# A decoder step on one core: a modulation unit multiplied in three visits instead of two, fewer constant products, and a later broadcast

## The chip, the cores and the metric

The kernel runs on one core of a Trainium2 chip. The metric is the device time in microseconds (us); of three runs of the kernel before, the median is 1660.69 us (1659.94 to 1660.98). TensorE (PE) multiplies, VectorE (DVE), ScalarE (ACT) and GpSimd (POOL) work elementwise, and SyncE (SP) issues nearly all DMA transfers, in its program order.

## What is computed

One inference step of a one-layer decoder for 288 tokens (256 of a prompt, 8 requests of 4 tokens), 2048 features. Only its beginning matters here: a conditioning vector per request is turned into shifts and scales by `w_ada`, the tokens are normalised and modulated, and the result is multiplied by `w_in`.

```python
mod = (jax.nn.silu(c) @ w_ada + b_ada).reshape(n, N_MOD, 1, D_MODEL)
sh_m, sc_m, gt_m, sh_f, sc_f, gt_f = [mod[:, i] for i in range(N_MOD)]
h = _rms(x, g_mix) * (1 + sc_m) + sh_m        # _rms: x * rsqrt(mean(x*x) + EPS) * gain
proj = h @ w_in
...                                           # convolution mixer and gating mixer, merged
x = x + gt_m * (merged @ w_out)
h2 = _rms(x, g_ffn) * (1 + sc_f) + sh_f
gate, up = jnp.split(h2 @ w_ffn_in, 2, axis=-1)
x = x + gt_f * ((jax.nn.silu(gate) * up) @ w_ffn_out)
```

## The kernel before

Tokens lie along the free dimension (288 columns); features lie in 16 tiles of 128 partitions. All weights, some 350 MB in float32, are read once, so a long stream of weight blocks is loaded while PE multiplies. Each float32 weight is split into a rounded part `hi` (a cast on ACT) and the rest `lo` (a subtraction on DVE), and a product is three matmuls: hi by hi, hi by lo, lo by hi.

The list `steps` is the order of the program. Its members are the following.

- **Units of modulation** (`Ada`, matmuls on L344): `aA` (4 loads of 512 KB) gives scale and shift of feature tile 0, `aB` (8 loads of 768 KB) those of tiles 1 to 3, `aC` those of tiles 4 to 7 (8 loads of 1 MB). A *visit* is a run of a unit's loads that PE multiplies one after another. All loads of a unit accumulate in one PSUM bank, and `tail` turns it into rows of `mod`. PE reads the raw data, so its buffer is free once PE has read it.
- **Blocks of `wA`** (matmuls on L448 for block 0, the class `FirstBlk`, and on L430 to L432 for blocks 1 to 8): feature tile 0 times eight output tiles each, 512 KB each. Blocks 0 to 5 use the raw x of tile 0 times its scale and are multiplied by the row factor later, on POOL (`rescale`); blocks 6 to 8 use the normalised tile 0, `h1[0]`. The raw buffer of a block is free once ACT and DVE have split it.
- **Blocks of `wB`, `wC`, `wE`, `wD`** and the rest of the layer follow.
- **The row factor**: `squares` (on ACT or POOL) of the 16 tiles of x, `sums1` (L504), which adds them up on PE, `sums1_out` and `rstd1` (L525, L528), and `norm1`, which broadcasts the row factor on PE (L202) and copies it to the tile `rb` (ACT).
- **`warm(n)`** (L234): n products of a constant tile of ones with itself, whose result nobody reads.

Five raw buffers (`RAW = 5`) serve the whole stream. At each step the load of the stream's member five places ahead is issued on SP; it waits until a buffer is free. Everything behind it on SP waits too.

Results of PE go to four PSUM accumulators `pm`. Each output tile of a block is copied out, odd ones by ACT and even ones by DVE (`sinkA`). Work that is to lie between the output tiles is hung on them by `at(block, j3=[...])`: it is issued behind the copy of tile 3. In this way each block also carries the splitting of the next one, `high` behind tiles 1 and 5, `low` behind tiles 2 and 6. `V` and `A` are pinned: DVE and ACT keep the written order here, so a copy can stand behind a cast that waits for a load.

Of the kernel before, what the change touches and what calls it, by code (L numbers as in the profile page):

```python
# [23 lines left out]
SEG = 4  # L24
# [52 lines left out]


def _body(tc, nc, d, pc, pw, pslot, ptmp, pps):
    ids = [0]  # L80

    def nm(s):
        ids[0] += 1
        return f"{s}_{ids[0]}"
# [4 lines left out]
    def slot(dt=F32, shape=(P, T)):  # L89
        return pslot.tile(list(shape), dt, tag="s", name=nm("s"), padded_shape=[P, TU])  # L90
# [29 lines left out]
    V, A, G, PE, SY = Pinned(nc.vector), Pinned(nc.scalar), nc.gpsimd, nc.tensor, nc.sync  # L120
# [18 lines left out]
    def load_x(a, b):  # L139
        SY.dma_start(x[:, a:b, :], d["x"][:, a:b, :])  # L140

    def load_consts():
        SY.dma_start(cp, d["cpack2"])
        SY.dma_start(masks[96:], d["cpack2"][:32, C_MASKS : C_MASKS + 32])
# [80 lines left out]
    def in_order(i):  # L225
        if S["strict"]:
            S["pe"] = i
        return i

    def warm(n, after=None):  # L230
        ps = psmisc()
        with behind(after):
            for _ in range(n):
                PE.matmul(ps[:, :P], ones, ones, start=True, stop=True)  # L234
# [82 lines left out]
    class Ada(Step):  # L317
# [15 lines left out]
        def run(self):  # L333
            w, ks = self.nq * 128, self.ks
            if self.blk == 0:
                Ada.cur[self.name] = pps.tile([P, 512], F32, tag="ada", name=nm("ada"), bufs=1)
            acc = Ada.cur[self.name]
            for k in range(self.nk // ks):
                for j in range(4):
                    kt = self.blk * self.nk + k * ks + j % ks  # L340
                    o = (k * 4 + j) * w
                    with behind(S.get("pe")):
                        self.last = in_order(
                            PE.matmul(  # L344
                                acc[32 * j : 32 * j + 32, :w],
                                cs[:, kt, :],
                                self.raw[:, o : o + w],
                                start=(kt < ks),
                                stop=(kt >= 16 - ks),
                                tile_position=(0, 32 * j),  # L350
                                skip_group_check=True,
                            )
                        )
            if (self.blk + 1) * self.nk == 16 and not self.defer:
                self.tail()
# [80 lines left out]
    class FirstBlk(Blk):  # L436
        def run(self):
            ah, al = self.rhs(0)
            g = SEG
            for m0 in range(0, self.nm, g):  # L440
                pss = [psmain() for _ in range(g)]
                for n in range(3):
                    for i, ps in enumerate(pss):
                        wh, wl = self.parts[m0 + i]
                        w, a = ((wh, ah), (wl, ah), (wh, al))[n]
                        with behind(S.get("pe")):
                            self.last = in_order(
                                PE.matmul(ps[:, : self.n], w, a, start=n == 0, stop=n == 2)  # L448
                            )
                for i, ps in enumerate(pss):  # L450
                    self.sinks(m0 + i, ps)

    class KBlk(Blk):
        def run(self):
# [30 lines left out]
    def ada(name):  # L485
        u = units[name]
        return [Ada(u, b) for b in range(16 // u[3])]
# [4 lines left out]
    def square(k, eng):  # L492
        q = sq[k] = slot()
        if eng is A:
            A.activation(q, x[:, k, :], AF.Square)
        else:
            G.tensor_tensor(q, x[:, k, :], x[:, k, :], ALU.mult)
# [72 lines left out]
    def gain1(k0, k1):  # L570
        V.scalar_tensor_tensor(
            gm1[:, k0:k1, :],
            mod[:, 16 + k0 : 16 + k1, :],
            1.0,
            gmix[:, k0:k1].unsqueeze(2).to_broadcast([P, k1 - k0, NC]),
            ALU.add,
            ALU.mult,
        )
# [246 lines left out]
    aA, aB, aC, aE = (ada(n) for n in ("aA", "aB", "aC", "aE"))  # L825
    wA = [FirstBlk("wA", 0, xe.__getitem__, sinkA, TU)]
# [3 lines left out]
    wC = [Blk("wC", i, rh1, sinkC) for i in range(RAWX // 2)]  # L830
    wE = [Blk("wE", i, rh1, sinkC) for i in range(RAWX // 4, 18)]
    mo = [Modulate(k, gm1, 0, "rb1", h1) for k in range(16)]

    def at(blk, **acts):
        for j, f in acts.items():
            blk.then.setdefault(int(j[1:]), []).extend(f)
# [6 lines left out]
    wA[0].defer = wB[0].defer = True  # L843

    def squares(*ks):
        return [lambda k=k, e=(G if k in (3, 5, 7, 9, 10, 12, 14, 15) else A): square(k, e) for k in ks]

    at(wA[0], j3=squares(0, 3, 5), j7=squares(1))
    at(wA[1], j3=squares(2), j7=squares(4))
    at(wA[2], j3=squares(6, 7, 9, 10), j7=squares(8))  # L850
    at(wA[3], j3=squares(11, 12, 14, 15), j7=squares(13))
    at(wA[4], j0=[sums1_out], j2=[rstd1])
    at(wA[6], j0=[aB[-1].tail], j3=[lambda: gain1(1, 4)], j5=[mo[1].affine], j7=[mo[1].high])
    at(wA[7], j0=[mo[1].low], j3=[mo[2].affine], j6=[mo[2].high])
    at(wA[8], j0=[mo[2].low], j2=[mo[3].affine], j5=[mo[3].high], j6=[mo[3].low])
# [5 lines left out]
    def free():  # L861
        V.on = A.on = False

    def h1_0():
        mo[0].norm()
        mo[0].affine()
        mo[0].high()
        mo[0].low()

    def norms():  # L870
        for k in range(1, 4):
            mo[k].norm()

    steps = [Do(silu), Do(lambda: warm(17)), *aA[:2], Do(lambda: warm(3, aA[1].last)), aA[2]]
    steps += [Do(lambda: warm(2, aA[2].last)), aA[3], Do(lambda: warm(1, aA[3].last)), Do(aA[3].tail), Do(early0)]
    steps += [Do(lambda: warm(4, aA[3].last))] + wA[:4] + [Do(sums1), wA[4], Do(norm1)] + aB[:4] + [Do(h1_0), wA[5]]
    steps += aB[4:] + [Do(norms)] + wA[6:] + [Do(free), wB[0]] + aC[:4] + wB[1:3] + aC[4:]
    steps += [wB[3], gain(4, 8), mk_h1(4, 5), mk_h1(5, 6), wB[4], mk_h1(6, 7), mk_h1(7, 8), rescale(0, 8), wB[5]]
    steps += [rescale(8, RAWX)] + weave(wC, visits(aE, 4, gain(8, 16)), 1, 13)[:-6]
# [39 lines left out]
    n = len(steps)  # L919
# [14 lines left out]
    for s in steps:  # L934
        if isinstance(s, Do):
            s.run()
            continue
        i = pos[id(s)]
        if i + AHEAD < len(stream):
            nx = stream[i + AHEAD]  # L940
            nx.load()
            if nx in pieces:
                load_x(*pieces[nx])
            if nx is wA[3]:
                SY.dma_start(ident, d["cpack2"][:, C_ID : C_ID + P])
            if nx is wA[8]:
                load_consts()
        while (
            nxt < len(blks)
            and blks[nxt].raw is not None  # L950
            and nxt <= cur + 1
            and not (blks[nxt].defer and blks[nxt] is not s)
        ):
            blks[nxt].split()
            nxt += 1
        s.run()
        if isinstance(s, Blk):
            cur += 1
# [112 lines left out]
```

## Time and profile before

| | before |
|---|---|
| median of the runs | 1660.69 us |
| the profiled execution, time | 1661.07 us |
| the profiled execution, span | 1659.2 us |
| HBM read | 352.56 MB |

The span runs from the first to the last instruction; some 1.9 us lie around it. In the slices of the page (one digit is a tenth of busy time in a fortieth of the span, 41.5 us) PE shows 8 in the second slice, 7 in the last and 9 in all others:

```profile
PE   9899999999999999999999999999999999999997
PEclk9999999999999999999999999999999999999998
```

The second slice, from 41 to 83 us, holds idle time. The costliest groups are the three matmuls of a product, 3704 of each:

```profile
L430 PE MATMUL pm<-s,hi 128*128 128x288 f32 (+1 forms) x3704 | 1097.5, 296 | 8.6 <-ACT s L113 8.0
L431 PE MATMUL pm<-s,hi 128*128 128x288 f32 (+1 forms) x3704 | 1094.2, 295 | 0.3 <-DVE s L113 0.3
```

Behind the count stand busy time, mean ns of one, and the time for which the engine was idle just before them, with what ended it. Matmuls overlap, so 296 ns is the length of one and not the distance between two, which is 133 to 140 ns here.

### The profile page before, as it was taken

How to read it: one execution, taken by the hardware profiler on the slowest of the kernel's cores; microseconds unless marked ns; L12 is line 12 of the kernel's file. 1: busy time of each engine (PE TensorE's matmuls, PEld its weight loads, DVE VectorE, ACT ScalarE, POOL GpSimd, SP SyncE). 2: the span in 40 equal slices, each digit the busy share in tenths (PEclk: the TensorE clock that was granted, in tenths of full speed). 3: DMA queues.
4: the chain of work that ended last, by engine and by line, in shares of the span. 5: the costliest groups of instructions: out<-in, count | busy, mean ns of one | idle time of the engine just before them, and what ended most of it. 6: DMA issues, size and time to landing. Idle time of an engine off the chain costs nothing.

```text
span 1659.2 us, 31266 instructions
## 1 busy us (share of the span) xinstructions
PE 1634.1 (98%) x12472; PEld 1562.1 (94%) x12472; DVE 986.8 (59%) x1993; ACT 734.7 (44%) x1370; POOL 120.7 (7%) x251
## 2 busy tenths in 40 slices
PE   9899999999999999999999999999999999999997
PEld 7688899989898999999999899999999999999997
DVE  4575567877765557557844455555555555555565
ACT  4343344643344434446733344444444444444453
POOL 2059000010100000002300000000000000000000
PEclk9999999999999999999999999999999999999998
DMA  7877864566777776674466755444454444544352
GB/s 289 308 286 286 338 213 175 177 250 249 278 307 278 281 285 246 255 267 156 153 254 254 301 170 195 173 158 141 157 205 161 170 138 155 201 166 168 126 172 76
DMA packets 57473, 357.66 MB, mean 216 GB/s; under 512 B 6528, under 2 KB 8992, under 8 KB 25328
## 3 DMA queue, kind: packets, MB, share of 16 engines
q1 hardware_dynamic: 56976, 354.95, 58.5%
q8 instruction: 97, 1.59, 0.4%
q0 software_dynamic: 352, 0.73, 0.1%
q14 instruction: 48, 0.39, 0.1%
HBM read 352.56 MB, written 3.09 MB: 214 GB/s over the span
## 4 chain that ended last, share of the span: by engine, by line
issue 50%; DVE 0%; ACT 0%; PE 0%; POOL 0%; POOLq 0%; DVEq 0%
DVE x L113 0%; PE px L202 0%; ACT t L113 0%; POOLq L1057 0%; POOL t L275 0%; ACT hi L113 0%; ACT s L113 0%; DVEq L1057 0%; POOL t L276 0%
## 5 line engine op out<-in xcount | busy, mean ns | idle before, releaser
L430 PE MATMUL pm<-s,hi 128*128 128x288 f32 (+1 forms) x3704 | 1097.5, 296 | 8.6 <-ACT s L113 8.0
L431 PE MATMUL pm<-s,hi 128*128 128x288 f32 (+1 forms) x3704 | 1094.2, 295 | 0.3 <-DVE s L113 0.3
L432 PE MATMUL pm<-s,lo 128*128 128x288 f32 (+1 forms) x3704 | 1094.1, 295 | 0.3 <-DVE lo L113 0.2
L113 DVE TENSOR_TENSOR lo<-raw,hi 128x512 fp32r<-128x512 f32 (+1 forms) x972 | 659.8, 686 | 481.3 <-ACT hi L113 467.6
L113 ACT CAST hi<-raw 128x512 fp32r<-128x512 f32 (+1 forms) x972 | 583.7, 607 | 797.3 <-PE pm L431 653.4
L430 PEld LDWEIGHTS pm<-s,hi 128*128 128x128 f32 x3704 | 697.6, 188 | 28.1 <-issue 12.0
L432 PEld LDWEIGHTS pm<-s,lo 128*128 128x128 f32 x3704 | 697.0, 188 | 1.1 <-DVE lo L113 1.1
L431 PEld LDWEIGHTS pm<-s,hi 128*128 128x128 f32 x3704 | 697.2, 188 | 0.6 <-DVE s L113 0.6
L344 PE MATMUL ada<-raw,cs 128*32 128x512 f32 (+3 forms) x896 | 90.5, 540 | 1.1 <-DMA raw<-in_aC 1.1
L113 DVE TENSOR_TENSOR s<-pm,s 128x288 f32<-128x288 f32 x120 | 54.5, 456 | 39.0 <-PE pm L432 38.7
L344 PEld LDWEIGHTS ada<-raw,cs 128*32 128x32 f32 x896 | 26.3, 111 | 47.5 <-issue 42.5
L196 POOL TENSOR_TENSOR r<-r,mhalf 128x3 f32<-128x3 f32 x3 | 2.8, 923 | 865.7 <-DVE r L113 865.7
L113 DVE TENSOR_TENSOR s<-t,s 128x288 fp32r<-128x288 f32 (+1 forms) x109 | 51.2, 471 | 12.0 <-ACT s L113 11.9
L113 ACT CAST s<-t 128x288 fp32r<-128x288 f32 (+1 forms) x109 | 47.1, 433 | 20.8 <-DVE t L113 16.4
L113 DVE SCALAR_TENSOR_TENSOR t<-t,pm 128x288 f32<-128x288 f32 x84 | 37.9, 451 | 25.2 <-PE pm L432 25.2
L562 POOL TENSOR_TENSOR s<-s,rb 128x288 f32<-128x288 f32 x48 | 43.0, 896 | 0.0
L113 DVE SCALAR_TENSOR_TENSOR x<-pm,mod,x 128x256 f32<-128x256 f32 x80 | 38.0, 476 | 0.0
L113 DVE SCALAR_TENSOR_TENSOR s<-pm,s 128x288 f32<-128x288 f32 x48 | 24.6, 512 | 15.2 <-PE pm L432 15.0
L113 DVE TENSOR_TENSOR t<-pm,mod 128x32 f32<-128x32 f32 x80 | 15.4, 192 | 29.5 <-PE pm L432 29.4
L239 POOL TENSOR_TENSOR t<-x,gm 128x32 f32<-128x32 f32 x16 | 7.4, 462 | 323.7 <-DVE gm L113 278.5
L275 POOL TENSOR_TENSOR t<-s,gm 128x32 f32<-128x32 f32 x28 | 12.0, 427 | 173.9 <-DVE s L113 103.4
L113 DVE SCALAR_TENSOR_TENSOR s<-s,pm 128x288 f32<-128x288 f32 x32 | 14.5, 454 | 15.2 <-PE pm L432 15.2
(122 smaller groups left out, 519.9 us busy)
## 6 DMA issues: line engine op xcount, KB each, us to landing
raw<-in_fi SPq DMA_DIRECT2D x84, 1024.0 KB, 4.8
raw<-in_a SPq DMA_DIRECT2D x64, 1024.0 KB, 6.3
raw<-in_f SPq DMA_DIRECT2D x64, 704.0 KB, 4.1
raw<-in_wD SPq DMA_DIRECT2D x36, 1024.0 KB, 5.2
raw<-in_wC SPq DMA_DIRECT2D x24, 896.0 KB, 6.0
raw<-in_aE SPq DMA_DIRECT2D x16, 1024.0 KB, 8.7
raw<-in_wo SPq DMA_DIRECT2D x16, 1024.0 KB, 7.3
raw<-in_aC SPq DMA_DIRECT2D x8, 1024.0 KB, 7.9
```

The lines of the kernel that those rows point to most:

```text
L113: i = f(*args, **kw)
L196: G.tensor_tensor(r, r, mhalf, ALU.pow)
L239: G.tensor_tensor(sam(a[:, TP:T]), sam(x[:, k, TP:]), bc4(gm[:, k, 1:]), ALU.mult)
L275: G.tensor_tensor(sam(h[:, TP:]), sam(t[:, TP:]), bc4(gm[:, k, 1:]), ALU.mult)
L344: PE.matmul(acc[32 * j : 32 * j + 32, :w], cs[:, kt, :], self.raw[:, o : o + w], start=(kt < ks), stop=(kt >= 16 - ks), tile_position=(0, ...
L430: PE.matmul(ps[:, : self.n], wh, ah, start=first, stop=False)
L431: PE.matmul(ps[:, : self.n], wh, al, start=False, stop=False)
L432: self.last = in_order(PE.matmul(ps[:, : self.n], wl, ah, start=False, stop=last))
L562: G.tensor_tensor(a[:, :T], a[:, :T], S["rb1"], ALU.mult)
```

## The change

It has six parts, all in the first hundred microseconds. The unit `aB` is multiplied in visits of two, two and four loads (before block 4's sum of squares, behind block 4, behind block 5) instead of four and four (behind block 4, behind block 5). The sum of squares stands behind the first visit, the broadcast `norm1` behind the second. The normalisation of tile 0 for blocks 6 to 8 (`mo[0]`) is hung on the output tiles of block 5 instead of standing ahead of it. Block 0 takes its output tiles two together and then one by one, instead of four and four. The constant products are 10, 1, 2, 1, 5 instead of 17, 3, 2, 1, 4. The squares are dealt out anew, eight on POOL as before, and the constants' load (`cp`, 236 KB) is asked for at a later step.

```diff
     class FirstBlk(Blk):
         def run(self):
             ah, al = self.rhs(0)
-            g = SEG
-            for m0 in range(0, self.nm, g):
-                pss = [psmain() for _ in range(g)]
+            cuts = [0] + list(range(2, self.nm + 1))
+            for a, b in zip(cuts, cuts[1:]):
+                pss = [psmain() for _ in range(a, b)]
...
     def squares(*ks):
-        return [lambda k=k, e=(G if k in (3, 5, 7, 9, 10, 12, 14, 15) else A): square(k, e) for k in ks]
-
-    at(wA[0], j3=squares(0, 3, 5), j7=squares(1))
+        return [lambda k=k, e=(G if k in (6, 7, 8, 9, 10, 12, 14, 15) else A): square(k, e) for k in ks]
+
+    at(wA[0], j3=squares(0), j7=squares(1))
     at(wA[1], j3=squares(2), j7=squares(4))
-    at(wA[2], j3=squares(6, 7, 9, 10), j7=squares(8))
+    at(wA[2], j3=squares(3, 6, 7, 8), j7=squares(5, 9, 10))
     at(wA[3], j3=squares(11, 12, 14, 15), j7=squares(13))
     at(wA[4], j0=[sums1_out], j2=[rstd1])
+    at(wA[5], j0=[mo[0].norm], j2=[mo[0].affine], j4=[mo[0].high], j6=[mo[0].low])
...
-    def h1_0():
-        mo[0].norm()
-        mo[0].affine()
-        mo[0].high()
-        mo[0].low()
-
...
-    steps = [Do(silu), Do(lambda: warm(17)), *aA[:2], Do(lambda: warm(3, aA[1].last)), aA[2]]
+    steps = [Do(silu), Do(lambda: warm(10)), *aA[:2], Do(lambda: warm(1, aA[1].last)), aA[2]]
     steps += [Do(lambda: warm(2, aA[2].last)), aA[3], Do(lambda: warm(1, aA[3].last)), Do(aA[3].tail), Do(early0)]
-    steps += [Do(lambda: warm(4, aA[3].last))] + wA[:4] + [Do(sums1), wA[4], Do(norm1)] + aB[:4] + [Do(h1_0), wA[5]]
+    steps += [Do(lambda: warm(5, aA[3].last))] + wA[:4] + aB[:2] + [Do(sums1), wA[4]] + aB[2:4] + [Do(norm1), wA[5]]
     steps += aB[4:] + [Do(norms)] + wA[6:] + [Do(free), wB[0]] + aC[:4] + wB[1:3] + aC[4:]
...
-            if nx is wA[8]:
+            if nx is wC[1]:
                 load_consts()
```

SP, from the identity to block 7 of wA. First before: `raw_170` is block 4, `raw_493` block 5, `raw_601` block 6.

```order
L945 DMA ident<-in_cpack 128x128
L394 DMA raw_170<-in_wA 128x1024
L328 DMA raw_212<-in_aB 128x1536
L328 DMA raw_278<-in_aB 128x1536
L143 DMA cp<-in_cpack 128x472
L328 DMA raw_340<-in_aB 128x1536
L144 DMA masks<-in_cpack 32x32
L328 DMA raw_408<-in_aB 128x1536
L394 DMA raw_493<-in_wA 128x1024
L328 DMA raw_566<-in_aB 128x1536
```

The same place in the changed kernel, where `raw_266` is block 4 and `raw_468` block 5; `raw_161`, `raw_204`, `raw_328` and `raw_400` are the first four loads of aB.

```order
L940 DMA ident<-in_cpack 128x128
L328 DMA raw_161<-in_aB 128x1536
L328 DMA raw_204<-in_aB 128x1536
L394 DMA raw_266<-in_wA 128x1024
L328 DMA raw_328<-in_aB 128x1536
L328 DMA raw_400<-in_aB 128x1536
L143 DMA cp<-in_cpack 128x472
L394 DMA raw_468<-in_wA 128x1024
L328 DMA raw_475<-in_aB 128x1536
L328 DMA raw_498<-in_aB 128x1536
```

Two loads of aB have moved ahead of block 4, and `cp` from between aB's second and third load to behind the fourth.

PE, from block 4's last tile to block 5's first. Before, `pm_554` is block 4's tile 7 and `pm_603` block 5's tile 0:

```order
L432 MATMUL pm_554<-s_197,lo_466 128x298
L202 MATMUL px_560<-ident,r_519 128x128 x3
L344 MATMUL ada_568<-raw_212,cs 32x384 x4
L344 MATMUL ada_568<-raw_278,cs 32x384 x4
L344 MATMUL ada_568<-raw_340,cs 32x384 x4
L344 MATMUL ada_568<-raw_408,cs 32x384 x4
L430 MATMUL pm_603<-s_197,hi_509 128x298
```

In the changed kernel, where `pm_559` is block 4's tile 7 and `pm_585` block 5's tile 0:

```order
L432 MATMUL pm_559<-s_188,lo_458 128x298
L344 MATMUL ada_470<-raw_328,cs 32x384 x4
L344 MATMUL ada_470<-raw_400,cs 32x384 x4
L202 MATMUL px_577<-ident,r_524 128x128 x3
L430 MATMUL pm_585<-s_188,hi_514 128x298
```

Two of the four loads are left here, and the broadcast has gone behind them; the other two (`raw_161`, `raw_204`) now stand between block 3 and the sum of squares.

ACT, from the copy of the broadcast into block 5. Before, `hi_615` is the first half of block 6 and `s_629` the copy of block 5's tile 3:

```order
L113 COPY rb_564<-px_560 128x288
L113 ACTIVATE t_593<-s_591,mod,gm_90 128x256
L113 CAST s_597<-t_593 128x288
L113 COPY s_613<-pm_609 128x298
L113 CAST hi_615<-raw_601 128x512
L113 COPY s_629<-pm_625 128x298
```

In the changed kernel `hi_599` is the first half of block 6 and `s_617` the copy of tile 3:

```order
L113 COPY rb_581<-px_577 128x288
L113 COPY s_597<-pm_593 128x298
L113 CAST hi_599<-raw_583 128x512
L113 ACTIVATE t_609<-s_591,mod,gm_90 128x256
L113 COPY s_617<-pm_613 128x298
L113 CAST s_625<-t_609 128x288
```

The modulation of tile 0 (`ACTIVATE`, then the cast) has moved from ahead of block 5's copies to behind the cast of block 6.

More of the change, by code (lines that the diff above doesn't have):

```diff
@@ L438, in run @@
             ah, al = self.rhs(0)
-            g = SEG
-            for m0 in range(0, self.nm, g):
-                pss = [psmain() for _ in range(g)]
+            cuts = [0] + list(range(2, self.nm + 1))
+            for a, b in zip(cuts, cuts[1:]):
+                pss = [psmain() for _ in range(a, b)]
                 for n in range(3):
                     for i, ps in enumerate(pss):
-                        wh, wl = self.parts[m0 + i]
-                        w, a = ((wh, ah), (wl, ah), (wh, al))[n]
+                        wh, wl = self.parts[a + i]
+                        w, r = ((wh, ah), (wl, ah), (wh, al))[n]
                         with behind(S.get("pe")):
                             self.last = in_order(
-                                PE.matmul(ps[:, : self.n], w, a, start=n == 0, stop=n == 2)
+                                PE.matmul(ps[:, : self.n], w, r, start=n == 0, stop=n == 2)
                             )
                 for i, ps in enumerate(pss):
-                    self.sinks(m0 + i, ps)
+                    self.sinks(a + i, ps)
     class KBlk(Blk):
```

## The prediction

> **What bounds the kernel now.** I read the page first, then the windows, then the timeline of the one stretch in which TensorE stands still.
>
> ```profile
> span 1659.2 us, 31266 instructions
> PE 1634.1 (98%) x12472; PEld 1562.1 (94%) x12472; DVE 986.8 (59%) x1993; ACT 734.7 (44%) x1370; POOL 120.7 (7%) x251
> 200.00:1640.00 1440.00, 1439.82 (x10920) 1392.36 (x10913) 864.71 (x1755) 655.61 (x1206) 43.34 (x117) 1.00 0.57 205
> ```
>
> From 200 to 1640 us TensorE (PE) is busy for 1439.82 of 1440 us at full clock. No DMA, VectorE (DVE) or ScalarE (ACT) wait shows there, and the diff adds no product. So whatever start of that stretch moves, the end moves by the same amount. The change can act only in the first hundred microseconds.
>
> ```profile
> 34.00:36.00 2.00, 1.49 (x11) 1.25 (x9) 0.18 (x1) 0.83 (x3) 0.00 (x0) 1.00 0.02 8
> 36.00:38.00 2.00, 1.11 (x6) 0.87 (x7) 1.94 (x5) 1.28 (x4) 0.86 (x1) 1.00 0.00 0
> 38.00:40.00 2.00, 2.00 (x25) 0.99 (x27) 0.46 (x1) 0.93 (x2) 0.41 (x2) 1.00 0.48 89
> 44.00:46.00 2.00, 0.23 (x2) 0.00 (x0) 0.00 (x0) 0.00 (x0) 0.00 (x0) 1.00 0.98 399
> ...
> 43.94 0.29 PE L432 MATMUL pm<-s,lo 128*128 128x298 f32 x1
> 51.53 0.62 PE L430 MATMUL pm<-s,hi 128*128 128x298 f32 x1 [7.30 <-ACT s L113]
> 52.58 3.97 PE L344 MATMUL ada<-raw,cs 128*32 128x384 f32 x32
> 56.48 0.40 PE L430 MATMUL pm<-s,hi 128*128 128x288 f32 x1
> ...
> 50.55 0.62 ACT L113 CAST hi<-raw 128x512 fp32r<-128x512 f32 x1 [7.88 <-DMA raw<-in_wA]
> 51.08 0.71 ACT L113 COPY s<-pm 128x298 f32<-128x298 f32 x2
> ```
>
> In a window row the columns are length, busy time of PE, PE weight load, DVE, ACT and POOL, then granted clock, DMA share and GB/s. PE stops at 43.94 and resumes at 51.53: 7.3 us. It waits for ACT to empty an accumulator, and ACT, in program order, waits for the raw data of block 6 of wA (50.5). The transfers idle from 34 to 38.5 us (8, 0, 89 GB/s), then run flat out while PE stands. So the ring of five buffers was full of loads that nobody read.
>
> ```profile
> 30.55 0.33 SPq L394 DMA_DIRECT2D raw<-in_wA  x1
> 37.96 3.01 SPq L328 DMA_DIRECT2D raw<-in_aB  x4
> 41.29 13.18 SPq L394 DMA_DIRECT2D raw<-in_wA  x3
> ...
> 29.55 2.15 PE L504 MATMUL px<-s,ones 128*32 128x288 f32 x32
> 31.63 0.41 PE L430 MATMUL pm<-s,hi 128*128 128x298 f32 x1
> 36.15 0.41 PE L430 MATMUL pm<-s,hi 128*128 128x298 f32 x1 [0.66 <-ACT s L113]
> 37.57 0.93 PE L202 MATMUL px<-ident,r 128*128 128x128 f32 x6 [0.74 <-POOL r L528]
> 38.44 2.79 PE L344 MATMUL ada<-raw,cs 128*32 128x384 f32 x32
> 41.16 0.41 PE L430 MATMUL pm<-s,hi 128*128 128x298 f32 x1
> ```
>
> SyncE (SP) issues block 5 at 30.55 and nothing until 37.96. The four held loads are aB's first four, 768 KB each, which PE reads only from 38.44 on. Five loads are then issued (four of aB, 512 KB of block 6), 3.67 MB, landing at 50.5.
>
> **The change, part by part.** *Two visits of aB ahead of the sum of squares* are the part that acts. They empty two buffers after block 3 instead of after block 4, so block 5 and two more loads of aB start while block 4 is multiplied. After block 4 only three loads are left ahead of the stall, 2.10 MB instead of 3.67 MB. I replay the path.
>
> *Where block 3 ends.* Loads run one behind another at the head:
>
> ```profile
> 20.00:22.00 2.00, 2.00 (x16) 2.00 (x16) 1.94 (x6) 1.91 (x6) 1.32 (x3) 1.00 1.03 426
> 22.00:24.00 2.00, 2.00 (x16) 2.00 (x15) 1.87 (x4) 1.91 (x6) 1.62 (x2) 1.00 1.00 420
> 21.25 2.38 POOL L497 TENSOR_TENSOR s<-x 128x288 f32<-128x288 f32 x3 [0.68 <-DMA x<-in_x]
> 23.40 0.62 ACT L113 CAST hi<-raw 128x512 fp32r<-128x512 f32 x1
> ```
>
> The last piece of x lands at 21.2. Behind it now stand the identity (64 KB), two loads of aB and only then block 4: 2112 KB, 2.16 MB, at 0.42 MB/us 5.1 us, so block 4 lands at 26.3. ACT's casts had nothing to wait for here (23.40). Now the cast of block 4 waits until 26.3, during block 3. As in the stall above, PE gets seven tiles ahead and then needs the copy behind that cast: 1.0 us from the landing to PE (50.55 to 51.53), one tile 0.42, so block 3 ends at 27.7. This needs block 3 to have come that far by 26.
>
> *The head.* The constant products go from 27 to 19 and the first block goes two tiles and then one by one:
>
> ```profile
> 1.06 7.00 PE L234 MATMUL px<-ones 128*128 128x128 f32 x34 [1.06 <-DVE ones L113]
> 7.98 1.08 PE L344 MATMUL ada<-raw,cs 128*32 128x128 f32 x32
> 5.29 0.24 DVE L113 TENSOR_SCALAR cs<-ctt 128x144 f32<-128x144 f32 x1
> 13.99 0.82 PE L448 MATMUL pm<-s,hi 128*128 128x298 f32 x4 [0.51 <-ACT s L113]
> 16.46 0.89 PE L448 MATMUL pm<-s,hi 128*128 128x298 f32 x4 [0.57 <-DVE s L113]
> ```
>
> Thirty-four records of products end near 7.8; twenty end near 5.5, just when cs is there (5.53). The head can thus begin 0 to 2.4 us earlier, the loads of aA permitting, and I take 1.4. The one-by-one order takes out the 0.57 us before 16.46, and moving POOL's squares away from DVE's first subtractions some tenths more. Block 3, from 25.3 now, would start near 23. All this is given back at block 4's landing: it ends at 27.7 if the head gains 1.4 or more, near 29 if it gains nothing. I use 27.7 and keep 29 for the range. ACT keeps two squares to a block, and POOL again ends its eight some 3 us after x.
>
> *From there to the landing of block 6.* Two visits of aB, 0.68 us each (2.72 us for four, 38.44 to 41.16): 29.1. The sum of squares takes 2.1: 31.2, against 31.63. Block 4 takes 4.35 (31.63 to 36.65, less the 0.66 waited): 35.6. That wait goes because block 5 is issued near 28.5 and not at 30.55. The next two visits end at 36.9, and the broadcast (0.87) no longer waits for POOL, which worked under those visits: 37.8. Seven tiles of block 5: 40.8. The third load of aB in the ring is read at 36.3 and frees its buffer: SP then issues aB's last two loads, and block 6 at 37. How long do these take?
>
> ```profile
> raw<-in_aB SPq DMA_DIRECT2D x1, 768.0 KB, 4.3
> raw<-in_wA SPq DMA_DIRECT2D x1, 512.0 KB, 9.2
> ```
>
> The first of the five landed 4.3 us after issue, block 6 9.2 us after its own, 12.6 after the first issue. Without 1.57 MB at 0.41 MB/us that is 8.8 us: landing at 45.1. If they flow without gaps, 4.3 plus 1.31 MB, 7.5 us: 43.8. I take 44.4, between.
>
> *Tile 0's normalisation inside block 5.* Its four steps leave the path between broadcast and block 5, where they lay beside aB's products anyway, so their old place saves nothing. In the new place ACT's affine stands between the cast of block 6 and the copy PE waits for:
>
> ```profile
> 39.47 0.60 ACT L113 ACTIVATE t<-s,mod,gm 128x256 f32<-128x256 f32 x1 [0.53 <-DVE s L113]
> ```
>
> It takes 0.60 us alone; rows of ACT that follow one another overlap by a tenth (50.55 plus 0.62 is 51.17, the copy starts at 51.08). I charge 0.5: PE resumes at 44.4 + 1.5 = 45.9. DVE's and POOL's shares lie under the stall.
>
> *After the stall.* Now: 56.48 - 51.53 = 4.95 us for one tile and four visits, part of it at half clock.
>
> ```profile
> 51.61:55.02 3.41, 3.41 (x19) 1.45 (x23) 2.75 (x7) 1.11 (x3) 0.00 (x0) 0.50 0.20 34
> 34.54:37.96 3.42, 2.02 (x13) 1.53 (x13) 2.11 (x5) 2.11 (x5) 0.86 (x1) 1.00 0.00 0
> 89.16:92.57 3.41, 1.56 (x19) 0.67 (x19) 0.54 (x6) 1.09 (x3) 0.00 (x0) 1.00 1.00 384
> 92.57:95.98 3.41, 3.41 (x13) 3.17 (x14) 2.57 (x5) 2.56 (x6) 1.14 (x2) 0.50 1.02 423
> ```
>
> The 3.49 us from 51.53 to 55.02 at half clock are 1.75 of work; the rest is 1.46; so 3.3 us at full clock. The grant changes on a grid of 3.41 us: a stretch with 1.56 us of work was followed by half clock, one with 2.02 was not. A stall of 5 us still brings half clock from 44.78. If the stretch to 48.20, with 2.3 us of work, lifts it, 1.15 us are lost and block 6 starts at 50.3, 6.1 earlier than 56.48. If only the next lifts it, it starts at 52.0, 4.4 earlier. The second dip (92.57 to 95.98, 1.7 us lost) comes from the waits around aC's last visits. Moved by 4.4 us those waits split over two stretches of the grid (over 2.1 us of work each) and the dip goes: 4.4 + 1.7 = 6.1. Moved by 6.1 us they fall mostly into one, and it stays: 6.1. Both ways lead to about 6.1.
>
> The Trainium skill ("TensorE: Matmul & The Clock Gate", Part 1: The HAM clock gate) says that the window of activity runs freely and that an idle window throttles. By its rule only the long stall would throttle; here a stretch 46% busy did, so the measurement goes ahead of the page.
>
> *The constants' load* moves behind aB's fourth load. It costs 0.24 MB, 0.6 us of transfer, and DVE's two copies from it wait in its program order (they waited 1.2 us before):
>
> ```profile
> 26.87 0.25 DVE L113 COPY zs<-cp 128x16 f32<-128x16 f32 x2 [1.20 <-DMA cp<-in_cpack]
> ```
>
> It lands at 26.3 plus two loads and itself, 4.4 us: 30.7. DVE has no other work until block 4's first tile, at 31.6. So nothing; if that cover is gone, what it lands after 32 stalls PE one to one.
>
> **Sum.** The profiled execution took 1661.07 (span 1659.2), 0.4 above the median of the runs, 1660.69. Minus 6.1: span 1653.1, and a median of 1654.6.
>
> **Rivals.** *Better by the clock*, 0.15: if the transfers take 7.5 us, the clock is lifted at the first chance and the second dip goes too, 6.7 + 1.7 = 8.4: 1652.3. Against it: the shift must suit the grid. *Head slow, half the gain*, 0.14: fewer constant products leave PE at half clock into the first block, block 3 ends at 29 or later, the landing slips by 1.3 and more, the clock is lifted late and the second dip stays: 4.4 - 1.3 = 3.1, or 1657.6. A row of L448 with steps of 0.28 instead of 0.14 us would show it. The same page and section of the Trainium skill asks for a busy window before the full clock and so speaks for this rival; the 20 records and the visits of aA right behind them speak against it. *No effect*, 0.06: the transfer is hidden or bound anyway, with the idle 4 us taken up by the loads moved ahead; then block 6 lands near 50 again and the time is within 1660 to 1661. Against it are the five loads after block 4, now three. *Slower*, 0.05: block 4 stands behind aB's first two loads, and everything to block 6 hangs on its landing one to one (44.4 follows 26.3). Were it to land after 32.4, all gain would be gone, each microsecond more costing one; at 36.5 the time is 1664.8. For this the full queue of the head would have to lose a third of its rate.
>
> **Chances and range.** The forecast, 4.5 to 7.7 us gained, has 0.60. Over 0.2% (3.3 us, about what a measurement can tell from no change): 0.60 + 0.15 + 0.10 of the half gain = 0.85; within it 0.04 + 0.06 = 0.10; slower 0.05. The range takes the forecast, most of the better case and the half gain: 1651.6 to 1657.7.
>
> **What would show it.** The transfers keep over 200 GB/s from 26 to 36 us, ACT waits near 24 to 26 for block 4, the long wait of PE falls to 4 to 5.5 us and begins near 41, and block 6 of wA starts at 50 to 52 us. The prediction is wrong if block 4's raw data lands much after 26.3, if the last three loads take over 9 us, or if the clock dips more often than now.

## The result and the profile after

The changed kernel took 1649.99 us (median of four runs, 1649.82 to 1654.28) beside 1660.84 us of the kernel before on the same chip (1659.94 to 1661.91): ratio 0.9941, 95% interval 0.9923 to 0.9958. That is 10.85 us less where 6.1 were forecast, and 1.6 us below the lower end of the range. On a second chip (the runs below) it was 1651.82 beside 1660.26, ratio 0.9953 (0.9938 to 0.9968), 8.4 us less. The first interval (7.0 to 12.8 us less) does not hold the 6.1, the second (5.3 to 10.3) does, and 1651.82 lies just inside the range.

The page of the changed kernel, its span and TensorE's (PE's) busy time:

```profile
span 1648.0 us, 31236 instructions
PE 1624.7 (99%) x12456; PEld 1553.4 (94%) x12456; DVE 987.8 (60%) x1993; ACT 733.3 (44%) x1370; POOL 121.5 (7%) x251
```

The timeline of the changed kernel (start, length, engine, line, operation, tiles; in brackets the idle time before it and what ended it), the rows that answer to those of the prediction:

```profile
26.15 0.62 ACT L113 CAST hi<-raw 128x512 fp32r<-128x512 f32 x1 [1.90 <-DMA raw<-in_wA]
27.75 1.50 PE L344 MATMUL ada<-raw,cs 128*32 128x384 f32 x16
29.06 2.12 PE L504 MATMUL px<-s,ones 128*32 128x288 f32 x32
30.36 0.25 DVE L113 COPY zs<-cp 128x16 f32<-128x16 f32 x2 [1.41 <-DMA cp<-in_cpack]
31.12 0.41 PE L430 MATMUL pm<-s,hi 128*128 128x298 f32 x1
...
37.43 0.38 PE L430 MATMUL pm<-s,hi 128*128 128x298 f32 x1
...
44.10 0.62 ACT L113 CAST hi<-raw 128x512 fp32r<-128x512 f32 x1 [5.14 <-DMA raw<-in_wA]
44.62 0.60 ACT L113 ACTIVATE t<-s,mod,gm 128x256 f32<-128x256 f32 x1
45.12 0.39 ACT L113 COPY s<-pm 128x298 f32<-128x298 f32 x1
45.56 0.62 PE L430 MATMUL pm<-s,hi 128*128 128x298 f32 x1 [4.96 <-ACT s L113]
46.61 3.84 PE L344 MATMUL ada<-raw,cs 128*32 128x384 f32 x32
50.37 0.40 PE L430 MATMUL pm<-s,hi 128*128 128x288 f32 x1
...
83.06 1.07 PE L344 MATMUL ada<-raw,cs 128*32 128x256 f32 x16 [0.38 <-DMA raw<-in_aC]
84.62 0.44 PE L364 MATMUL px<-ident,ev 128*128 128x128 f32 x2 [0.49 <-ACT ev L113]
...
447.45 0.40 PE L430 MATMUL pm<-s,hi 128*128 128x288 f32 x1 [0.81 <-ACT hi L113]
```

Down to 50.37 the replay of the prediction stands: block 4's raw data is cast at 26.15 (forecast 26.3), the first visits begin at 27.75 (27.7), the sum of squares at 29.06 (29.1), block 4 at 31.12 (31.2), block 5 at 37.43 (37.8). The cast of block 6 starts at 44.10 (44.4), PE resumes at 45.56 (45.9), block 6 starts at 50.37 (50.3).

The windows of the changed kernel (length, busy time of PE, weight load, DVE, ACT, POOL, then clock, DMA share, GB/s):

```profile
30.00:32.00 2.00, 2.00 (x26) 1.27 (x19) 0.41 (x3) 0.40 (x1) 0.00 (x0) 1.00 0.81 254
32.00:34.00 2.00, 2.00 (x18) 2.00 (x17) 1.07 (x3) 1.28 (x3) 0.00 (x0) 1.00 0.77 294
34.00:36.00 2.00, 2.00 (x21) 1.44 (x23) 1.76 (x5) 1.40 (x4) 0.86 (x1) 1.00 0.98 391
36.00:38.00 2.00, 2.00 (x22) 1.38 (x15) 0.24 (x1) 0.28 (x1) 0.00 (x0) 1.00 0.63 137
38.00:40.00 2.00, 2.00 (x16) 2.00 (x15) 1.30 (x3) 0.53 (x2) 0.49 (x2) 1.00 0.96 393
45.37:48.78 3.41, 3.22 (x19) 1.55 (x23) 2.90 (x8) 1.70 (x5) 0.00 (x0) 0.50 0.09 14
93.00:96.00 3.00, 3.00 (x25) 3.00 (x24) 2.77 (x6) 1.67 (x4) 0.85 (x2) 1.00 0.84 328
187.98:1638.43 1450.45, 1447.52 (x11002) 1398.08 (x11000) 866.41 (x1766) 656.67 (x1210) 44.74 (x118) 1.00 0.57 204
```

The transfers that stood at 8, 0 and 89 GB/s from 34 to 40 us now run at 391, 137 and 393. One stretch at half clock follows the stall, and the second one (92.57 to 95.98 before) is not there. The last row is the PE-bound stretch, from the 11,000th PE instruction before the last to the last. The same instructions in the kernel before, and its last visit of aC:

```profile
196.75:1649.44 1452.69, 1450.63 (x11002) 1401.41 (x11000) 867.84 (x1766) 657.97 (x1210) 44.20 (x118) 1.00 0.56 204
```

```profile
89.99 1.07 PE L344 MATMUL ada<-raw,cs 128*32 128x256 f32 x16 [1.10 <-DMA raw<-in_aC]
```

The first is a window, the second a row of the timeline. As many instructions take 2.24 us less. So the difference between the two profiled executions grows along the program:

| place on PE | before | after | shift |
|---|---|---|---|
| first product of block 0 | 13.99 | 12.29 | -1.70 |
| sum of squares | 29.55 | 29.06 | -0.49 |
| end of the stall | 51.53 | 45.56 | -5.97 |
| block 6 | 56.48 | 50.37 | -6.11 |
| transposes behind aC (L364) | 91.55 | 84.62 | -6.93 |
| 11,000 instructions before the end | 196.75 | 187.98 | -8.77 |
| last product | 1649.44 | 1638.43 | -11.01 |

Up to block 6 it is the forecast's 6.1. Behind it come 0.7 at aC's last visit (the idle time in brackets falls from 1.10 to 0.38), 1.7 from the missing stretch at half clock, and 2.24 in the PE-bound stretch, in which the kernel before waits for nothing.

### The profile page after: what moved, and what is told of

The parts are those of the page before. It is cut to its first block, busy times and chain, and to the rows that moved or that the text cites. A ratio compares the mean times of both kernels' runs of the same rounds, so it can differ in the third digit from the quotient of the medians.

```text
span 1648.0 us, 31236 instructions
## 1 busy us (share of the span) xinstructions
PE 1624.7 (99%) x12456; PEld 1553.4 (94%) x12456; DVE 987.8 (60%) x1993; ACT 733.3 (44%) x1370; POOL 121.5 (7%) x251
## 4 chain that ended last, share of the span: by engine, by line
issue 50%; DVE 0%; ACT 0%; POOL 0%; PE 0%; POOLq 0%; DVEq 0%
DVE x L113 0%; ACT t L113 0%; PE px L202 0%; POOLq L1052 0%; POOL t L275 0%; ACT hi L113 0%; ACT s L113 0%; DVEq L1052 0%; POOL t L276 0%
## 5 line engine op out<-in xcount | busy, mean ns | idle before, releaser
L113 DVE TENSOR_TENSOR s<-pm,s 128x288 f32<-128x288 f32 x120 | 54.3, 454 | 37.8 <-PE pm L432 37.3
L344 PEld LDWEIGHTS ada<-raw,cs 128*32 128x32 f32 x896 | 26.3, 111 | 48.1 <-issue 42.2
L113 DVE SCALAR_TENSOR_TENSOR t<-t,pm 128x288 f32<-128x288 f32 x84 | 37.8, 450 | 25.0 <-PE pm L432 25.0
```

Of the source, the lines that this page charges most:

```text
L113: i = f(*args, **kw)
L344: PE.matmul(acc[32 * j : 32 * j + 32, :w], cs[:, kt, :], self.raw[:, o : o + w], start=(kt < ks), stop=(kt >= 16 - ks), tile_position=(0, ...
```

## The experiments

Each kernel was timed against the kernel before on the same chip. Beside the time stands the **step**: the mean distance between the starts of two successive products (lines 430 to 432, pairs less than 160 ns apart), over the last 1530 us of the profile, some 10,500 pairs. It is good to 0.01 ns; so much depends on where the count begins. It is 132.59 ns in the profile of before and 132.25 after.

### The change cut in two, and both kernels again

The kernels before and after as they are; the visits alone, without the squares, the constants, the first block and tile 0's normalisation:

```
-wA[:4] + [Do(sums1), wA[4], Do(norm1)] + aB[:4] + [Do(h1_0), wA[5]]
+wA[:4] + aB[:2] + [Do(sums1), wA[4]] + aB[2:4] + [Do(norm1), Do(h1_0), wA[5]]
```

and all the rest of the change without the visits:

```
-wA[:4] + aB[:2] + [Do(sums1), wA[4]] + aB[2:4] + [Do(norm1), wA[5]]
+wA[:4] + [Do(sums1), wA[4], Do(norm1)] + aB[:4] + [wA[5]]
```

> The kernel before, unchanged, for a second profile. Open is where 2.4 us of the 11 come from, which the changed kernel gains little by little between 110 and 1640 us: its products follow one another there every 132.3 ns instead of 132.8. Theory 'placement': the step belongs to the program (where its tiles lie), so this profile shows 132.8 again within 0.1 ns, stage by stage, and the time is 1660 to 1662. Rival 'run': the step differs from execution to execution, so this profile shows another mean, by 0.2 ns or more, and the times of the runs spread by 2 us or more without any change of the clock. Also: the half-clock stretches near 48 and 92 us shift with the grid of 3.41 us if that grid runs freely; where the one near 92 us is missing, the time is some 1.7 us lower.

> The changed kernel, unchanged, for a second profile. 'Placement': products every 132.3 ns again, time 1649.5 to 1651.5, or up to 1654.5 where the clock dips twice. 'Run': a mean step off by 0.2 ns or more. One of its four runs so far took 1654.28: if the clock alone makes that, a profile with a second dip, or a longer first one, shows the block behind the dip 1.7 us later for each 3.41 us of half clock.

> The kernel before with the visits of aB alone (two, two, four; sum of squares behind the first, broadcast behind the second); tile 0's normalisation stays ahead of block 5, and head, squares, first block and constants' load stay as before. Theory 'visits': they carry the whole gain of the start. Block 4 lands near 26.3, block 6 near 44 to 45.5, PE resumes 1.0 us later and block 6 starts at 50 to 51.5: 5 to 6.5 us earlier than before, time 1650 to 1655. Rival 'head': without the faster head block 3 ends near 29 and everything is 1 to 1.5 us later than in the changed kernel: block 6 starts at 51 to 52, time 1651 to 1656. Rival 'rest': under 2 us gained.

> The changed kernel with the visits put back (sum of squares, block 4, broadcast, then aB's first four, then block 5); everything else as changed. Theory 'visits': SP again issues nothing from about 28 to 36 us, the long wait of PE is back at 6.5 to 8 us and ends where block 6 lands. The head's 1.5 to 2.4 us are kept in part, since no load of aB stands before block 4: block 6 starts 1 to 3 us earlier than before (53.5 to 55.5), time 1657 to 1660. Rival 'rest': the time is under 1654.

| kernel | us | ratio (95%) | stall of PE | block 6 starts | step, ns |
|---|---|---|---|---|---|
| before again | 1659.63 | 0.9999 (0.9989 to 1.0008) | 43.27 to 51.05 | 55.82 | 132.59 |
| after again | 1651.82 | 0.9953 (0.9938 to 0.9968) | 40.43 to 46.41 | 51.31 | 132.25 |
| visits alone | 1655.07 | 0.9970 (0.9961 to 0.9979) | 43.74 to 46.60 | 52.28 | 132.59 |
| the rest | 1655.87 | 0.9975 (0.9965 to 0.9985) | 42.93 to 48.51 | 53.80 | 132.25 |

The visits alone bring 5.2 us of the 8.4, and they shorten the stall as told. Block 6 starts at 52.28 there, later than the 50 to 51.5 expected and close to the rival 'head': the stall ends 0.2 us later than in the changed kernel again, and the half clock behind it lasts until 51.57 instead of 49.81. The rest brings 4.4 although it leaves the stall 5.6 us long; 6.5 to 8 us of stall and 1657 to 1660 us were expected, and the rival, under 1654, did not come either. Together the two make 9.6, so the 8.4 are not a sum of two independent gains. The step goes with the rest, not with the visits, and it belongs to the program: two profiles of before agree in it, and two of after. Windows of the kernel before again:

```profile
92.60:96.00 3.40, 3.40 (x28) 3.40 (x27) 3.40 (x8) 2.16 (x5) 0.00 (x0) 1.00 1.02 427
194.16:1647.22 1453.06, 1451.03 (x11002) 1401.83 (x11000) 868.05 (x1766) 657.92 (x1210) 44.19 (x118) 1.00 0.56 203
```

and of the changed kernel again:

```profile
189.72:1639.91 1450.19, 1447.22 (x11001) 1398.01 (x11000) 866.71 (x1766) 657.52 (x1210) 44.71 (x118) 1.00 0.56 204
```

In the kernel before the second stretch at half clock is missing here; of the seven profiles of kernels with the visits of before, two have it. The grid of 3.41 us moves from one execution to the next: the clock first rose at 7.24 and 6.40 us in the two profiles of before, at 4.41 and 5.44 in those of after. The Trainium skill ("TensorE: Matmul & The Clock Gate", Part 1: The HAM clock gate) says that the window runs freely and is not reset by a kernel; these four agree. So the 1.7 us of that stretch belong to one execution of before, and the second pair of profiles shows the change without them: block 6 4.5 earlier, the end 7.3 earlier, 2.9 of it in the PE-bound stretch (1453.06 and 1450.19 us).

### What shortens the step

Two parts of the change, each alone in the kernel before. The constants:

```
-warm(17) ... warm(3, aA[1].last) ... warm(4, aA[3].last)
+warm(10) ... warm(1, aA[1].last) ... warm(5, aA[3].last)
```

and the squares:

```
-e=(G if k in (3, 5, 7, 9, 10, 12, 14, 15) else A)
+e=(G if k in (6, 7, 8, 9, 10, 12, 14, 15) else A)
-at(wA[0], j3=squares(0, 3, 5), j7=squares(1))
+at(wA[0], j3=squares(0), j7=squares(1))
-at(wA[2], j3=squares(6, 7, 9, 10), j7=squares(8))
+at(wA[2], j3=squares(3, 6, 7, 8), j7=squares(5, 9, 10))
```

> The kernel before with only the constant products of the change: 19 instead of 27 (10, 1, 2, 1, 5), all else as before, so every product behind the head has the operands in the places of before; it only stands eight instructions earlier in the program. Open is why successive products of the PE-bound stretch are 132.25 ns apart in the changed kernel and 132.59 in the kernel before (about 2.4 us over the stretch). Theory 'places of the moving operand': the step stays at 132.59 and only the head gains, first L448 1.4 to 1.7 us earlier, about 1658.8 us. Theory 'position or number of the instructions': the step falls to 132.25, about 1656.3 us.

> The kernel before with only the squares dealt anew between ScalarE and GpSimd and put at other tiles. By the order of the pool's slots this gives about a third of the last 9000 products another place of the moving operand (6084 of 9000 keep that of before, 8054 have that of the changed kernel). Theory 'places': the step falls to between 132.25 and 132.35, about 2 us, and the head gains up to 0.5 us by VectorE's first subtractions, about 1657.8. Theory 'position or number of the instructions': the step stays at 132.59, 1659.8 to 1660.3.

The constants alone: 1659.71 us, ratio 0.9999 (0.9989 to 1.0008), step 132.59. The squares alone: 1657.82, ratio 0.9984 (0.9974 to 0.9994), step 132.40, above the 132.25 to 132.35 expected. The same stretch of instructions, as a window of the kernel with the constants alone,

```profile
195.16:1648.28 1453.12, 1450.95 (x11001) 1401.74 (x11000) 867.05 (x1766) 657.27 (x1210) 44.17 (x118) 1.00 0.57 204
```

and of the kernel with the squares alone:

```profile
197.54:1647.65 1450.11, 1448.17 (x11001) 1399.19 (x11000) 866.72 (x1766) 657.80 (x1210) 44.89 (x118) 1.00 0.57 204
```

Eight instructions fewer change nothing in this stretch; the squares take 2.6 us off a stretch that begins over 150 us behind the last of them. Constants alone also answer for the head: the first product of block 0 stands at 12.31 instead of 13.99, and in the time nothing can be seen of it.

The squares do two things: other engines do them at other times, and one pool of buffers hands out its places in another sequence from there on. From this pool come the moving tiles, the operands that PE streams (`s` in `pm<-s,hi`), and also the squares and the results that ACT and DVE write. The next kernel, the kernel before with three lists turned, does only the second; every engine does the same squares in the same order:

```
-at(wA[0], j3=squares(0, 3, 5), j7=squares(1))
+at(wA[0], j3=squares(3, 5, 0), j7=squares(1))
-at(wA[2], j3=squares(6, 7, 9, 10), j7=squares(8))
+at(wA[2], j3=squares(7, 9, 10, 6), j7=squares(8))
-at(wA[3], j3=squares(11, 12, 14, 15), j7=squares(13))
+at(wA[3], j3=squares(12, 14, 15, 11), j7=squares(13))
```

As built, this program and the kernel before have the same instructions in the same order on every engine, with the same waits, and every operand outside the pool lies where it lay. Only addresses in the pool differ.

And the way back: the changed kernel with the squares dealt as before.

> The kernel before with three lists of squares only written in another order, such that each engine still works on the same squares in the same order: only the pool hands out other places, and of the last 9000 products 1452 read their moving operand from another place. Theory 'places': the mean step of successive products, 132.59 ns in three profiles of programs with the places of before, changes by at least 0.03 ns, up or down, though no engine's order changes. Rival 'the dealing of the squares itself (which engine does them, and when)': the step stays at 132.59 within 0.01. The time stays near 1660 either way, within 1 us.

> The kernel of the run places alone once more, now timed against the kernel before on one chip. In its one profile the step was 132.16 ns instead of 132.59 and the time 1655.89 beside 1659.70, with every engine's order as before. Theory 'the places set the step, in every execution': the step is 132.16 within 0.02 again, and 10,655 steps times 0.43 ns take 4.6 us off, so 3.5 to 5 us, a ratio of 0.997 to 0.998. Rival 'that execution was lucky': the time is within 1 us of before.

> The changed kernel with the squares dealt as before (engines and tiles), all else as changed. 2916 of the last 9000 products then read their moving operand from another place. Theory 'places, moved mostly by the dealing of the squares': the step rises from 132.25 by about what the squares alone took off, 0.18 ns, to 132.4 (between 132.35 and 132.6), 1.3 us; VectorE's first subtractions beside GpSimd's squares cost the head up to 0.5 more: about 1652.5 to 1653.5 beside 1651 to 1652 of the changed kernel. Rival 'the step comes from the visits or the constants': 132.25 stays.

Places alone: step 132.16 in both profiles, one run at 1655.89, then timed 1655.40 beside 1660.5, ratio 0.9971 (0.9960 to 0.9981). Its stretch, a window of the timed kernel's profile:

```profile
195.70:1644.23 1448.53, 1446.41 (x11001) 1397.23 (x11000) 867.69 (x1766) 657.85 (x1210) 44.27 (x118) 1.00 0.57 204
```

So 4.2 us come off this stretch by nothing but addresses in the pool; the time had been expected to stay within 1 us of 1660. With the old squares the changed kernel took 1653.00, ratio 0.9960 (0.9948 to 0.9971), as expected, but its step rose only to 132.30, less than the 132.35 to 132.6 expected. Of the last 9000 matmuls, 946 read their moving operand from another place there than in the kernel before, and the step is 0.29 ns shorter; with the squares alone it is 2916 of them and 0.19 ns. So the effects of places don't add up, nor do they go by how many places change. Places in PSUM can be left out: in the visits alone 4366 of the 9000 write to another one, and the step is 132.59. Windows of the changed kernel with the old squares show another loss:

```profile
447.18:450.59 3.41, 1.62 (x15) 0.48 (x7) 0.91 (x2) 1.56 (x3) 0.00 (x0) 1.00 0.93 387
450.59:454.00 3.41, 3.41 (x16) 3.39 (x17) 1.59 (x3) 1.72 (x4) 0.00 (x0) 0.50 1.01 428
```

PE waits 1.6 us for a load of wD (through the cast on ACT), and a stretch at half clock follows. The changed kernel waits 0.81 at the same place (447.45 above); the row of the kernel before shows no idle time:

```profile
456.28 0.40 PE L430 MATMUL pm<-s,hi 128*128 128x288 f32 x1
```

This is what gives part of the shorter step back: within the stretch of the windows the distances of successive products add up to 1332.48 us before and 1329.22 after, 3.26 less (0.13 of it is one pair that is more than 160 ns apart after), and all else in it takes 1.0 longer, 0.8 of it this wait.

### What is left of the stall

The affine of tile 0 (the `ACTIVATE` that applies its scale and shift) ahead of the cast of block 6:

```
-at(wA[5], j0=[mo[0].norm], j2=[mo[0].affine], j4=[mo[0].high], j6=[mo[0].low])
+wA[5].then[0] = [mo[0].norm, mo[0].affine]
+at(wA[5], j4=[mo[0].high], j6=[mo[0].low])
```

four pairs of visits instead of two, two and four (the steps for tiles 1 to 3 go one block later, spread over blocks 7 and 8):

```
-steps += aB[4:] + [Do(norms)] + wA[6:] + ...
+steps += aB[4:6] + [wA[6]] + aB[6:] + [Do(norms)] + wA[7:] + ...
```

and, on top of the affine's edit, block 6 loaded right behind block 5, with the multiplications in the order of the change:

```
+loads = [s for s in stream if s is not wA[6]]
+loads.insert(loads.index(aB[4]), wA[6])
...
-nx = stream[i + AHEAD]
+nx = loads[i + AHEAD]
```

> The changed kernel with tile 0's affine put ahead of the cast of block 6 on ScalarE (norm and affine both behind the first tile of block 5). By the prediction's charge of 0.5 us the copy for which PE waits comes 1.0 us after the landing of block 6 instead of 1.54, so the stall ends 0.5 us earlier and the time falls by 0.5 us, to about 1651.3 beside 1651.8 on this chip (a fifth of a per cent is more than can be told by the time, the trace tells it). Rival: the affine waits there for VectorE's norm and the broadcast, holds up ScalarE's copies of block 5, and PE stalls earlier by as much: no change. The step stays at 132.25, since no place changes.

> The changed kernel with the last four visits split too: two behind block 5, two behind block 6, so that block 6's load stands ahead of aB's last two loads; the tail of aB, the gain and tiles 1 to 3 follow one block later. Theory 'what is left of the stall is the two loads queued ahead of block 6': block 6 lands near 40.5 instead of 44.0, the stall falls from 5 to under 1.5 us, the half clock behind it goes or is shorter, block 6 starts 3 to 4 us earlier by the PE work in front of it (about 46 with two visits less ahead of it, 1.4 us), and the time falls by 3 to 5 us, to about 1647.5 on this chip. Rival: the later tail leaves ScalarE and VectorE too little time before the first block of the next stream (tiles 1 to 3 in 7 us instead of 10), and PE waits there 2 to 4 us: the time stays at 1650 to 1652.

> The changed kernel with the affine ahead of the cast (as in the run affine first) and with block 6 loaded right behind block 5, ahead of aB's last four loads; the multiplications keep their order. Theory 'the stall is block 6's place in the queue and nothing else': block 6 lands before 36 us, the stall of 4 to 5 us in block 5 goes, PE walks into the last four visits near 41 and waits there at most 2 us for aB's last loads (landing by 44), no half clock follows, block 6 starts near 44.5 to 46 instead of 49.4 to 50.4; if all of that came through, 4 to 5 us, 1646 to 1647. Rival 'behind it the transfers are the bound': the loads up to aC's last visit (near 84 us) are no sooner there, PE waits longer at that place (0.8 to 1.2 us now), and only 1 to 2 us come through: 1649 to 1650.

| kernel | us | ratio (95%) | stall of PE | block 6 starts | L364 | step, ns |
|---|---|---|---|---|---|---|
| affine first | 1650.68 | 0.9946 (0.9931 to 0.9960) | 40.54 to 44.48 | 49.41 | 84.06 | 132.25 |
| four pairs | 1651.22 | 0.9947 (0.9932 to 0.9961) | 40.49 to 43.72 | 47.29 | 84.42 | 132.36 |
| block 6 loaded first | 1646.85 | 0.9925 (0.9908 to 0.9941) | none | 45.73 | 80.18 | 132.25 |

The timeline of the affine's kernel:

```profile
43.50 0.62 ACT L113 CAST hi<-raw 128x512 fp32r<-128x512 f32 x1 [3.79 <-DMA raw<-in_wA]
44.03 0.40 ACT L113 COPY s<-pm 128x298 f32<-128x298 f32 x1
...
44.48 0.60 PE L430 MATMUL pm<-s,hi 128*128 128x298 f32 x1 [3.65 <-ACT s L113]
```

From the cast to PE it is 0.98 us instead of 1.46 (44.10 to 45.56): the charge of 0.5 was right. In the time it can't be told. Four pairs land block 6 at 42.2, not at the expected 40.5, and the time stays, as the rival said. Block 6 starts 3.1 us earlier than in the changed kernel, but 1.4 of these are the two visits that now stand behind it, 0.55 are the products of aB's tail, which have moved into block 7, and 0.8 goes in block 8, in gaps of PE of some tenths of a microsecond; the rival had named a wait of 2 to 4. A longer step costs another microsecond. Block 6 loaded first, its timeline:

```profile
41.65 2.14 PE L344 MATMUL ada<-raw,cs 128*32 128x384 f32 x24
44.95 0.85 PE L344 MATMUL ada<-raw,cs 128*32 128x384 f32 x8 [1.16 <-DMA raw<-in_aB]
45.73 0.40 PE L430 MATMUL pm<-s,hi 128*128 128x288 f32 x1
...
78.62 1.07 PE L344 MATMUL ada<-raw,cs 128*32 128x256 f32 x16 [0.61 <-DMA raw<-in_aC]
```

PE walks from block 5 into the visits, waits 1.16 us for aB's last load, and no half clock follows. Nearly all comes through: L364 stands 4.4 us earlier than in the changed kernel, with the wait for aC 0.2 longer, and 3.9 earlier than in affine first, beside which its edit moves one load and nothing else. The rival, that the transfers up to aC bound this anyway, falls. The time is 13 us less than before, and 3 to 5 less than that of the changed kernel by their ratios (0.9925 beside 0.9941 and 0.9953). No run timed the two on one chip, and their intervals overlap in part; it is the trace that shows the gain.

The last kernel is this one with three lists of squares turned (`6, 7, 8, 3`, `9, 10, 5` and `12, 14, 15, 11`), each engine's order the same:

> The kernel of the run block 6 loaded first with three lists of squares written in another order, each engine's work and order the same, only other places (some 1450 of the last 9000 products). Theory 'the places set the step': the start of the kernel up to 180 us is as in that run within 0.5 us, the step moves off 132.25 by 0.03 ns or more, in a direction that none of the runs lets one foresee, and the time moves from 1646.85 by 10.7 us for each ns of it. Rival 'places matter only in the arrangement of before': step 132.25 and 1646.85 stay.

It took 1648.87 us, ratio 0.9931 (0.9917 to 0.9944), the step is 132.48, and the start is the same (block 6 at 45.73, L364 at 80.01). The PE-bound stretch of the run before and of this one:

```profile
183.51:1634.59 1451.08, 1447.78 (x11001) 1398.60 (x11000) 866.77 (x1766) 657.21 (x1210) 44.25 (x118) 1.00 0.56 204
183.59:1635.34 1451.75, 1449.83 (x11002) 1400.85 (x11000) 867.52 (x1766) 657.36 (x1210) 44.66 (x118) 1.00 0.56 204
```

The places move the step in this arrangement too, here upwards by 0.23 ns. In the time it can't be told: the intervals overlap, and in the profile only 0.7 of the 2.5 us show, since the wait at wD's load (1.77 us from start to start there) is gone again.

## Why the prediction was wrong

- **"Whatever start of that stretch moves, the end moves by the same amount"** is the step that failed. The row behind it shows that PE is busy, not how long one product takes, and the prediction put a change of that at nothing, since the diff adds no product. The diff deals the pool's places anew, by the squares and by other parts that were not taken apart, and successive products come 0.34 ns sooner on average. That is some 3.2 us in the stretch, of which 2.24 are kept in the first pair of profiles and 2.87 in the second. No case of the prediction held this. That places alone can do it is shown by the run places alone, which takes 5.1 us off the median (0.9971).
- **The second half-clock stretch, "both ways lead to about 6.1"**: failed as well. At a shift of 6.1 the stretch was gone, 1.7 us more, as in the rival by the clock. But the kernel before runs without it in another execution, too. Reading it off one execution's grid was the error; the phase of the grid can't be read from a profile for the next run.
- **aC's last visit**: 0.7 us less wait than before in the first pair of profiles, not in the sum.
- **The visits as the part that acts**: right. Alone they bring 5.2 us, and in the first profile the replay to block 6 is right within 0.4 us at each point. That the stall lasts 5 us and brings half clock is right too. So is its cause, block 6's place in the queue: with its load moved, and nothing else beside the run affine first, the stall goes.
- **Block 6, 6.1 us earlier**: within 0.02, but luck in part. PE resumed 0.34 sooner than forecast, the half clock from 45.56 to 48.78 cost 1.61 instead of 1.15, and the work behind the stall is 3.2 by the prediction's own terms (1.75 and 1.46), not 3.3. In the second pair half clock lasted for two stretches, and block 6 is 4.5 earlier, the prediction's other case (4.4).
- **The head given back at block 4's landing**: right. The first product came 1.70 earlier (1.4 taken), and 0.49 was left at the sum of squares. The constants alone bring nothing in the time, though not for this reason: no load of aB stands ahead of block 4 there, and the sum of squares comes 1.25 earlier.
- **The affine, 0.5 us**: right, 0.48.
- **The constants' load, nothing**: right. DVE's copies end at 30.61, ahead of block 4's first tile.
- **The rivals**: better by the clock came in part, as told. Head slow is ruled out by full clock from 4.41 us on, ahead of block 0; no effect, by block 6's landing at 44.1; slower, by block 4's data, there at 26.15, 6 us ahead of the point from which that decides.

The prediction's 6.1 and the stretch's 2.24 make 8.3, and the medians on the second chip are 8.4 apart. That they meet is no proof: the profiles of that pair add up otherwise, 4.4 us at the start of the stretch and 2.9 in it. The first chip's 10.85 holds the missing half clock and aC's visit besides.

What stays open is which addresses in the pool make a product slower, and how. The distances go from 125 to 144 ns, and product by product they repeat: between the two profiles of before, 44 of 10,593 differ by more than 1 ns. Between before and places alone 5064 of 10,610 differ, and in 3232 of these both products read their moving operand from the same places as before. So the addresses of the two products themselves don't fix the distance, and no run isolates what does.

## What to carry to other kernels

When one engine is busy throughout, compare also the distance of its instructions, not only its waits: an edit that merely changes the sequence of allocations moved the whole program by three tenths of a per cent here, and in another arrangement it made the distance longer, so that it can be taken for the effect of the edit. Of a half-clock stretch in one profile ask another profile before it is booked as gain or loss. And where a ring of buffers fills with loads that are read late, move the one load that is waited for forward in the queue before reordering the multiplications.

## What the runs showed of the hardware

- The mean distance of the same 128x288 products is 132.16 to 132.59 ns by the places which the pool of moving tiles and results hands out, and it repeats to 0.01 ns in the three programs that were profiled twice.
- A grid stretch of 3.41 us with 1.62 us of PE work was followed by half clock at 450 us, as was one with 1.56 in the kernel before; 2.02 was not. In all fifteen profiles, counting the grid from the first rise of the clock, each stretch at full clock with up to 1.93 us of work (the visits alone, 41.33 to 44.74) was followed by half clock, and each from 1.98 us on (affine first, 82.08 to 85.49) by full clock.
- The phase of that grid differed between the two profiles of a program, so that the stall cost one stretch at half clock (45.37 to 48.78) in one execution of the changed kernel, where PE stood for 5.0 us, and two (42.99 to 49.81) in another, where it stood for 5.7.
